# A hybrid decoder layer on one core: disjoint token halves in the up projection, with the halo of the convolution computed by ScalarE

## The chip, the cores and the metric

The kernel runs on one core of a Trainium2 chip. The metric is the device time of one execution in microseconds (us); the time of a kernel is the median of several executions.

## The reference, cut to what matters

One decoder layer on 1024 tokens, with 16 meta tokens ahead of them, in float32. Attention and a recurrent mixer come first; their output is added to the residual h. What the change touches is the ConvFFN behind them: an up projection to 2 x 2816 channels, a causal depthwise convolution over three tokens, GELU times the other half, and a down projection.

```python
def conv_ffn(a, w_up, conv_w, conv_b, w_down):
    u = a @ w_up
    u = lax.conv_general_dilated(
        u, conv_w[:, None, :], window_strides=(1,), padding=[(CONV_WIDTH - 1, 0)], ...) + conv_b
    gate, up = jnp.split(u, 2, axis=-1)
    return (jax.nn.gelu(gate, approximate=True) * up) @ w_down
...
    a = rmsnorm(h, ln_ffn_pre[l])
    y = conv_ffn(a, w_ffn_up[l], ffn_conv_w[l], ffn_conv_b[l], w_ffn_down[l])
    h = h + rmsnorm(y, ln_ffn_post[l])
return h[:, N_META:, :]
```

Only the 1024 tokens are returned. The first of them needs u of the two tokens before it, so the up projection runs on 1026 columns: the last two meta tokens and the 1024 tokens.

## The kernel before, in words

The layer runs in stages: attention and mixer, output projection, up projection with convolution, down projection. Each float32 operand of a matmul is split into a rounded part (hi, made by a cast on ScalarE) and the rest (lo, made by a subtraction on VectorE or GpSimd), and each product is three matmuls: hi x hi, hi x lo, lo x hi. All elementwise instructions are recorded through a helper, so in the profile their line is L59; they are told apart by the names of their tiles. TensorE's order is that of the code. The other engines' instructions are put in order by a scheduler; each engine then works through its own queue strictly in that order, waiting on semaphores.

**The up projection.** The channels are cut into 22 blocks of 128 for the gate and 22 for the other half; `ft` counts them. The 1026 columns are cut into two units, `p` = 0 and 1, and each unit's columns into a left and a right half. Round 0 (`plain_unit`, L1392) multiplies directly. Each of the rounds 1 to 21 (`unit`, L1410, driven by the loop at L1544) takes the 2 x 2 blocks (gate and other half by the two halves of the 1024 input features; the two halves of the columns) by a scheme with 7 products instead of 8. A product has 12 matmuls: four blocks of 128 input features by three parts. The products are numbered j = 0 to 6, and in each j unit 0 goes first and unit 1 follows.

- Before the rounds, `t_sums` (L1290) makes the sums of column blocks that products 1, 2, 3 and 5 read, in place in `at2`; `t_split` (L1279) splits the seven into the tiles `t`.
- `prep` (L1163) loads the four weight blocks of the next round (`ra`), makes their four sums on GpSimd (`ws`) and splits all seven into `uh` (cast on ScalarE) and `ul` (subtraction on VectorE or GpSimd). One weight is prepared in each j.
- Product 0 goes into the PSUM bank `pa`; ScalarE copies it to `xu` (x1). Products 1, 3 and 5 add up in the bank `pb`, 2 and 6 in `pc`, and 4 adds to `pa`. Between products VectorE reads the banks: behind product 1 it makes u2 (second half of `xu`) from pb and x1, behind product 3 it makes u3 (tile `u`) from pb and x1 and then a half of `uu`, and later the other halves of `uu` and `ug`. So product 5 may begin only when VectorE has read pb for `u`.
- `gated` (L1385) runs a round later, for unit 0 in j = 1 and for unit 1 in j = 3. It convolves `ug` and `uu` (`conv`, L1376): one ACTIVATE on ScalarE makes tap 2 and the bias, two scalar_tensor_tensor on VectorE add taps 1 and 0 in the tile `c`. GELU on ScalarE, a product on GpSimd and a store to DRAM (`gsc`) follow.

**The columns before the change.** Unit 0 has columns 0 to 515 (two halves of 258), unit 1 columns 514 to 1025 (two halves of 256). The two columns 514 and 515 are in both, since the convolution of unit 1 begins two columns late: unit 0 gives 514 tokens, unit 1 gives 510.

Of the kernel before, what the change touches and what calls it, by code (L numbers as in the profile page):

```python
# [9 lines left out]
F32 = mybir.dt.float32  # L10
F32R = mybir.dt.float32r
# [6 lines left out]
P = 128  # L18
# [11 lines left out]
NEG = -3.0e38  # L30
GROUPS = [(0, 3), (3, 6), (6, 9)]
WN = [258, 256]
C0 = [0, 514]
FA, FH, FO = 840, 800, 740
WR = 4
WARM = 26
# [55 lines left out]
def layer_kernel(ctx: ExitStack, tc: tile.TileContext, x, meta, xt, relative, lbl, gpre, gpost, win,  # L92
# [1162 lines left out]
    def trans(i):  # L1255
        r, t0 = tok(i)
        a2 = a2t.pop(i)
        cs = slice(t0 - 14, t0 - 14 + r)
        for half in range(2):
            pt = ps_b(f"pa2_{i}_{half}")  # L1260
            for j in range(4):
                k = 4 * half + j
                T.transpose(pt[:, j * r:(j + 1) * r], a2[:r, P * k: P * (k + 1)], ident[:r, :r])
            pv = pt[:, : 4 * r].rearrange("p (k t) -> p k t", k=4)
            ks = slice(4 * half, 4 * half + 4)
            for p in range(2):
                lo_, hi_ = max(cs.start, C0[p]), min(cs.stop, C0[p] + 2 * WN[p])
                if lo_ < hi_:
                    A.copy(
                        at2[p][:, ks, lo_ - C0[p]:hi_ - C0[p]], pv[:, :, lo_ - cs.start:hi_ - cs.start])  # L1270

    tt = [[None] * 8 for _ in range(2)]

    def t_tiles(p, j, where, tag):
        tag, n, off = (tag + (8 * WN[p], 0)[len(tag) - 1:])[:3]
        both = where.tile([P, n], F32R, tag=tag, name=f"t{p}_{j}")[:, off:off + 8 * WN[p]].rearrange("p (a c) -> p a c", a=8)
        return both[:, 0:4], both[:, 4:8]

    def t_split(p, j, src, where, *tag):  # L1279
        hi, lo = t_tiles(p, j, where, tag)  # L1280
        marks["cast"] = A.copy(hi, src)
        marks["low"] = V.tensor_tensor(lo, src, hi.bitcast(F32), op=ALU.subtract)
        tt[p][j] = (hi, lo)

    def quarter(p, j):
        n = WN[p]
        a, c = {0: (0, 0), 7: (0, n), 4: (4, 0), 6: (4, n)}[j]
        return at2[p][:, a:a + 4, c:c + n]

    def t_sums(p, where, last):  # L1290
# [24 lines left out]
    for i in range(1, NBLK):  # L1315
        py = ps_b(f"py1_{i}")
        if i >= 3:
            marks["gain"] = y0_gain(i)
        if i == 1:
            load_xh(1)  # L1320
            load_xh(0)
        if i + 1 < NBLK:
            for n in range(i + 1 if i < 6 else i + 2, min(i + 2 if i < 5 else i + 3, NBLK)):
                second_load(n)
            load_xh(i + 1)
        run(blocks[i], py, wo, range(4), True, False)
        if i == 3:
            trans(1)
        run(blocks[i], py, wo, range(4, 7 if i == 1 else 8), False, i > 1)
        if i > 3:  # L1330
            trans(i - 2)
        if i == 5:
            trans(0)
        if i == 1:
            pm = ps_b("py1_0")
            for _ in meta_part(pm, wo, True):
                pass
            for p in range(3):
                out_last(p)
            run(k7(1), py, wo[KD - 1:], range(1), False, True)  # L1340
            post(1, py)
            ysum = xhs.pop("sum")
            for l in range(2):
                A.copy(ysum[:2, 512 * l:512 * l + 512], pm[32 * l:32 * l + 2])
            G.tensor_tensor(ysum[:2, :512], ysum[:2, :512], ysum[:2, 512:], op=ALU.add)
            for p in (3, 4):
                out_last(p)
            continue
        post(i, py)
        if i == 2:  # L1350
            post(0, ysum[:, :512], ysum[:, 512:])
        if i == 5:
            t_split(0, 0, quarter(0, 0), ep, "e0")
            t_split(0, 4, quarter(0, 4), ep, "e1")
        if i == 7:
            with tc.issue_after(marks["scale"].ins), tc.issue_after(marks["normed"].ins):
                t_split(0, 7, quarter(0, 7), mxp, "X2", MIX["X2"])
        if i == 8:
            t_split(0, 6, quarter(0, 6), mxp, "X1", MIX["X1"], 16)
        if i in (2, 3):  # L1360
            for p in (1 + 2 * i, 2 + 2 * i):
                out_last(p)
# [22 lines left out]
    def gated(ft, p, ug, uu):  # L1385
        cg = conv(ft, p, 0, ug)
        A.activation(cg, cg, AF.Gelu_apprx_tanh)
        cu = conv(ft, p, 1, uu)
        marks["mult"] = G.tensor_tensor(cg, cg, cu, op=ALU.mult)
        marks["store"] = SY.dma_start(gsc[P * ft: P * (ft + 1), C0[p]:C0[p] + 2 * WN[p] - 2], cg)  # L1390

    def plain_unit(p, bank):  # L1392
        n = WN[p]
        us = outputs(0, p)
        for col in range(2):
            for side in range(2):
# [9 lines left out]
                A.copy(us[side][:, col * n:(col + 1) * n], pt)  # L1406
                yield
        later.append((0, p, *us))

    def unit(ft, p, bank):  # L1410
# [6 lines left out]
        x1, u2 = pair[:, :n], pair[:, WN[0]:WN[0] + n]  # L1417
        u3 = xup.tile([P, WN[0]], F32, tag="u3", name=f"u3_{nm}")[:, :n]

        def mm(j, pt, first):  # L1420
            hi, lo = made[7 * ft + j]
            th, tl = tt[p][j]
            for k in range(4):
                s = slice(P * k, P * (k + 1))
                T.matmul(pt, hi[:, s], th[:, k], start=(first and k == 0), stop=False, skip_group_check=True)  # L1425
                T.matmul(pt, hi[:, s], tl[:, k], start=False, stop=False, skip_group_check=True)  # L1426
                T.matmul(pt, lo[:, s], th[:, k], start=False, stop=(k == 3), skip_group_check=True)  # L1427
# [347 lines left out]
```

## Time and profile before

| | |
|---|---|
| median of three runs | 1270.1 us (1269.75 to 1271.96) |
| profiled execution | 1270.04 us |
| its span, first to last instruction | 1268.2 us |
| mean granted TensorE clock | 0.999 |
| busy: TensorE, VectorE, ScalarE, GpSimd | 99%, 72%, 54%, 40% |
| up projection, rounds 1 to 21 | about 636 to 1048 us of the span |

How to read the rows quoted below. In a timeline, a row begins with the start in us from the span's start and the duration, then engine (PE is TensorE, DVE VectorE, ACT ScalarE, POOL GpSimd, SPq SyncE's DMA queue), line, operation, the tiles it writes and reads (out<-in), shapes and types, and how many alike were merged. In brackets stand the engine's idle time ahead of it and the instruction that, by the profile, ended the wait. Successive instructions of an engine are pipelined, so one can start a little before the last has ended. A matmul is shown with 0.28 us, though the next starts much sooner; starts, not durations, tell its cost.

### The profile page before, as it was taken

Reading aid. Unit: us, or ns where it says so; the run is one execution under the profiler, and the core shown is the slowest. Engines: PE = TensorE matmul, PEld = TensorE weight load, DVE = VectorE, ACT = ScalarE, POOL = GpSimd, SP = SyncE. Lnnn points to the kernel's source line nnn. Section 1 sums busy time; section 2 is a strip of 40 time slices with the busy share of each in tenths; the row PEclk is TensorE's granted clock in tenths of the full one; section 3 lists DMA queues with packets and bytes.
Section 4 is the critical chain, followed back from the end, with each engine's and each line's share of the span. In section 5 each row is a group of like instructions: output and inputs, shape, how many; then the busy total and the mean of one; then the engine's idle time right before and its main releaser. Section 6 shows DMA issues by size and latency. Waiting matters only on the chain.

```text
span 1268.2 us, 26069 instructions
## 1 busy us (share of the span) xinstructions
PE 1254.6 (99%) x10168; PEld 1174.9 (93%) x10168; DVE 912.7 (72%) x1504; ACT 685.4 (54%) x1632; POOL 512.0 (40%) x396
## 2 busy tenths in 40 slices
PE   9999999999999999999999999999999999999997
PEld 8999999999999998778999999999999998878886
DVE  6764646565655564558899888889898877797586
ACT  7765466547644763456764544544445544564554
POOL 5442323333213311353067677677676731020111
PEclk9999999999999999999999999999999999999999
DMA  8554564464633534787222222222222247955363
GB/s 322 170 104 100 98 140 83 98 125 118 115 99 68 125 94 128 237 278 273 85 76 72 80 92 68 92 92 68 92 77 75 76 136 259 343 184 167 92 216 125
DMA packets 117599, 169.30 MB, mean 133 GB/s; under 512 B 10258, under 2 KB 57938, under 8 KB 117476
## 3 DMA queue, kind: packets, MB, share of 16 engines
q1 hardware_dynamic: 94244, 156.10, 37.7%
q0 software_dynamic: 23232, 11.54, 7.7%
q8 instruction: 80, 1.31, 0.4%
q14 instruction: 43, 0.35, 0.1%
HBM read 138.50 MB, written 52.17 MB: 150 GB/s over the span
## 4 chain that ended last, share of the span: by engine, by line
PE 83%; DMA 6%; DVE 4%; ACT 3%; issue 1%; POOL 1%; SPq 1%; DVEq 0%; ACTq 0%; POOLq 0%
PE pb L1426 5%; PE pb L1425 5%; PE pb L1427 4%; PE pd L1600 4%; PE pd L1601 4%; PE pd L1599 4%; PE pa L759 3%; PE pa L1426 3%; PE pc L1426 3%; PE pa L1425 3%; PE pc L1425 3%; PE pc L1427 3%; PE pa L1427 3%; DMA ra<-in_wup_dram 2%; PE pt L735 2%; DMA gi<-gsc 1%
## 5 line engine op out<-in xcount | busy, mean ns | idle before, releaser
L1425 PE MATMUL pb<-t,uh 128*128 128x258 f32 x504 | 140.6, 279 | 0.8 <-DVE u L59 0.8
L1426 PE MATMUL pb<-t,uh 128*128 128x258 f32 x504 | 140.9, 280 | 0.3 <-DVE t L59 0.3
L1427 PE MATMUL pb<-t,ul 128*128 128x258 f32 x504 | 140.1, 278 | 0.0
L1600 PE MATMUL pd<-wl,gh 128*128 128x512 f32 (+1 forms) x312 | 121.0, 388 | 1.2 <-DVE wl L59 1.2
L1599 PE MATMUL pd<-wh,gh 128*128 128x512 f32 (+1 forms) x312 | 120.8, 387 | 0.5 <-DVE x L59 0.5
L1601 PE MATMUL pd<-wh,gl 128*128 128x512 f32 (+1 forms) x312 | 120.7, 387 | 0.0
L59 DVE SCALAR_TENSOR_TENSOR c<-uu,cwt,c 128x514 f32<-128x514 f32 (+1 forms) x88 | 106.9, 1215 | 0.0
L59 DVE SCALAR_TENSOR_TENSOR c<-ug,cwt,c 128x514 f32<-128x514 f32 (+1 forms) x88 | 101.5, 1154 | 0.0
L59 ACT ACTIVATE c<-c 128x514 f32<-128x514 f32 (+1 forms) x44 | 27.9, 634 | 130.1 <-DVE c L59 130.1
L1425 PEld LDWEIGHTS pb<-t,uh 128*128 128x128 f32 x504 | 94.8, 188 | 1.0 <-DVE u L59 1.0
L1426 PEld LDWEIGHTS pb<-t,uh 128*128 128x128 f32 x504 | 94.8, 188 | 0.6 <-DVE t L59 0.6
L1427 PEld LDWEIGHTS pb<-t,ul 128*128 128x128 f32 x504 | 94.8, 188 | 0.0
L1426 PE MATMUL pa<-t,uh 128*128 128x258 f32 (+1 forms) x336 | 93.9, 279 | 0.0
L1426 PE MATMUL pc<-t,uh 128*128 128x258 f32 (+1 forms) x336 | 93.9, 279 | 0.0
L1425 PE MATMUL pa<-t,uh 128*128 128x258 f32 (+1 forms) x336 | 93.6, 279 | 0.0
L1425 PE MATMUL pc<-t,uh 128*128 128x258 f32 (+1 forms) x336 | 93.6, 278 | 0.0
L1427 PE MATMUL pa<-t,ul 128*128 128x258 f32 (+1 forms) x336 | 93.4, 278 | 0.0
L1427 PE MATMUL pc<-t,ul 128*128 128x258 f32 (+1 forms) x336 | 93.4, 278 | 0.0
L59 POOL TENSOR_TENSOR ul<-ws,uh 128x512 fp32r<-128x512 f32 x42 | 69.2, 1647 | 59.6 <-PE pa L1427 43.9
L59 POOL TENSOR_TENSOR ws<-ra,ra 128x512 f32<-128x512 f32 x42 | 67.8, 1615 | 61.0 <-DMA ra<-in_wup_dram 33.9
L59 POOL TENSOR_TENSOR c<-c,c 128x514 f32<-128x514 f32 (+1 forms) x44 | 68.5, 1558 | 54.2 <-ACT c L59 49.5
L59 DVE TENSOR_TENSOR ul<-ra,uh 128x512 fp32r<-128x512 f32 x43 | 41.6, 967 | 46.6 <-POOL ul L59 46.6
(386 smaller groups left out, 4179.8 us busy)
## 6 DMA issues: line engine op xcount, KB each, us to landing
ra<-in_wup_dram SPq DMA_DIRECT2D x88, 256.0 KB, 2.6
mp<-msc SPq DMA_DIRECT2D x23, 512.0 KB, 5.6
tsc<-in_wdown_dram SPq DMA_DIRECT2D x44, 256.0 KB, 5.6
wi<-tsc SPq DMA_DIRECT2D x44, 256.0 KB, 3.0
gi<-gsc SPq DMA_DIRECT2D x33, 256.0 KB, 4.0
wi<-in_wdown_dram SPq DMA_DIRECT2D x33, 256.0 KB, 5.3
gsc<-c SPq DMA_DIRECT2D x22, 257.0 KB, 2.0
tsc<-in_wdown_dram POOLq DMA_DIRECT2D x22, 256.0 KB, 6.7
```

Of the source, the lines that this page charges most:

```text
L59: ins = call(*args, **kw)
L735: T.transpose(pt[:b, jj * r:(jj + 1) * r], pb[:r, 0, start(j):start(j) + b], ident[:r, :r])
L759: T.matmul(po[:, :P], w_, vn[:, j], start=(j == 0), stop=(j == i))
L1425: T.matmul(pt, hi[:, s], th[:, k], start=(first and k == 0), stop=False, skip_group_check=True)
L1426: T.matmul(pt, hi[:, s], tl[:, k], start=False, stop=False, skip_group_check=True)
L1427: T.matmul(pt, lo[:, s], th[:, k], start=False, stop=(k == 3), skip_group_check=True)
L1599: T.matmul(py, gh[:, s], wh, start=(k == 0 and pr not in (3, 7)), stop=False, skip_group_check=True)
L1600: T.matmul(py, gh[:, s], wl, start=False, stop=False, skip_group_check=True)
L1601: T.matmul(py, gl[:, s], wh, start=False, stop=(k == NH - 1), skip_group_check=True)
```

## The change

The units become disjoint. Unit 0 now has columns 0 to 513, in a left half of 258 (two meta columns and 256 tokens) and a right half of 256; unit 1 has columns 514 to 1025 as before. The two meta columns take part only in the products that make left halves: 0, 1, 4 and 5. Products 2, 3 and 6 of unit 0 have 256 columns; product 3 adds into pb from its column 2. For the meta columns product 1 reads the same operand as product 0, so the split tile gets these columns as a copy (ScalarE); the operand of product 5 gets one small extra subtraction (VectorE, 4 x 2 columns). A few sizes of padding (`gap`) and offsets of tiles change with the narrower tiles.

Both units now give 512 tokens. For unit 1 the convolution needs the last two columns of unit 0, which are no longer among its own. Tap 2 and the bias run over all 512 columns; then three ACTIVATEs on ScalarE, each on a single column, add taps 1 and 0 of the missing columns from unit 0's `ug` or `uu` (`before`), with the column of `c` itself as the bias and the tap as the scale. VectorE's two steps start one and two columns later (511 and 510 columns). Unit 0's `ug` and `uu` are kept in `lefts` until then.

```diff
-C0 = [0, 514]
+C0 = [0, 514, 1026]
+HALF = 256
...
+    def width(p, j):
+        return WN[p] if j in (0, 1, 4, 5) else HALF
...
     def t_split(p, j, src, where, *tag):
-        hi, lo = t_tiles(p, j, where, tag)
+        hi, lo = tt[p][j] = t_tiles(p, j, where, tag)
+        o = width(p, j) - src.shape[-1]
+        if o:
+            for x, y in zip((hi, lo), tt[p][0]):
+                A.copy(x[:, :, :o], y[:, :, :o])
+        hi, lo = hi[:, :, o:], lo[:, :, o:]
...
         V.tensor_tensor(b21, b21, b22, op=ALU.subtract)
+        if o:
+            V.tensor_tensor(m21, m21, m11, op=ALU.subtract)
...
-    def conv(ft, p, side, u):
+    def conv(ft, p, side, u, before):
         m = ft + NF * side
-        w = 2 * WN[p] - 2
-        c = cv.tile([P, 514], F32, tag=f"c{side}", name=f"c{side}_{ft}_{p}", bufs=2 if side else 3)[:, :w]
-        A.activation(c, u[:, 2:2 + w], AF.Identity, bias=cbt[:, m:m + 1], scale=cwt[:, m, 2:3])
-        V.scalar_tensor_tensor(c, u[:, 1:1 + w], cwt[:, m, 1:2], c, ALU.mult, ALU.add)
-        V.scalar_tensor_tensor(c, u[:, 0:w], cwt[:, m, 0:1], c, ALU.mult, ALU.add)
+        c = cv.tile([P, 514], F32, tag=f"c{side}", name=f"c{side}_{ft}_{p}", bufs=2 if side else 3)[:, :512]
+        taps = [cwt[:, m, t:t + 1] for t in range(3)]
+        o = 2 * (p == 0)
+        A.activation(c, u[:, o:o + 512], AF.Identity, bias=cbt[:, m:m + 1], scale=taps[2])
+        if p:
+            for t, dst, src in ((1, 0, 1), (0, 0, 0), (0, 1, 1)):
+                d = c[:, dst:dst + 1]
+                A.activation(d, before[:, 512 + src:513 + src], AF.Identity, bias=d, scale=taps[t])
+        for t in (1, 0):
+            c0 = c[:, 2 - t - o if not o else 0:]
+            V.scalar_tensor_tensor(c0, u[:, t if o else 0:][:, :c0.shape[-1]], taps[t], c0, ALU.mult, ALU.add)
         return c
...
     def plain_unit(p, bank):
...
-                pt = bank(f"pq{p}_{col}{side}")[:, :n]
+                w = HALF if col else n
+                pt = bank(f"pq{p}_{col}{side}")[:, :w]
...
     def unit(ft, p, bank):
...
             th, tl = tt[p][j]
+            pt = pt[:, pt.shape[-1] - width(p, j):]
...
-        pc = bank(f"pc{nm}")[:, :n]
+        pc = bank(f"pc{nm}")[:, :HALF]
         mm(2, pc, True)
         yield
         mm(3, pb, False)
-        V.tensor_tensor(u3, pb, x1, op=ALU.add)
-        marks["last"] = V.tensor_tensor(uu[:, n:2 * n], pc, u3, op=ALU.add)
+        V.tensor_tensor(u3, pb[:, o:], x1[:, o:], op=ALU.add)
+        marks["last"] = V.tensor_tensor(uu[:, right], pc, u3, op=ALU.add)
```

On the chip's queues the rounds keep their order but for the small ACTIVATEs. This is ScalarE's queue of before, in the passage from round 5 to round 6, where the convolution of round 5 begins (`c`, then channel block and unit; `uh` is the cast of a weight, from a loaded block `ra` or a sum `ws`; `xu` is the copy of product 0 of round 6):

```order
L59 ACTIVATE c_5_0_9337<-uu_0_9007,cbt,cwt 128x514
L59 CAST uh_9224<-ws_9222 128x512
L59 ACTIVATE c_5_1_9418<-uu_1_9025,cbt,cwt 128x510
L59 ACTIVATE c_5_0_9332<-ug_0_9006,cbt,cwt 128x514
L59 CAST uh_9264<-ra_11_9254 128x512
L59 ACTIVATE c_5_1_9413<-ug_1_9024,cbt,cwt 128x510
L59 COPY xu_0_9270<-pa_0_9272 128x258
L59 CAST uh_9345<-ws_9343 128x512
L59 COPY xu_1_9288<-pa_1_9290 128x256
```

The same passage of ScalarE's queue with the change:

```order
L60 ACTIVATE c_5_0_9368<-uu_0_9032,cbt,cwt 128x512
L60 CAST uh_9255<-ws_9253 128x512
L60 ACTIVATE c_5_1_9452<-uu_1_9050,cbt,cwt 128x512
L60 ACTIVATE c_5_1_9452<-uu_0_9032,c_5_1_9452,cwt 128x1 x3
L60 ACTIVATE c_5_0_9363<-ug_0_9031,cbt,cwt 128x512
L60 CAST uh_9295<-ra_11_9285 128x512
L60 ACTIVATE c_5_1_9444<-ug_1_9049,cbt,cwt 128x512
L60 ACTIVATE c_5_1_9444<-ug_0_9031,c_5_1_9444,cwt 128x1
L60 COPY xu_0_9301<-pa_0_9303 128x258
L60 ACTIVATE c_5_1_9444<-ug_0_9031,c_5_1_9444,cwt 128x1 x2
L60 CAST uh_9376<-ws_9374 128x512
L60 COPY xu_1_9319<-pa_1_9321 128x256
```

Three small ACTIVATEs stand ahead of the second pair of convolutions and of the cast from `ra`, one ahead of the first copy to `xu`, two ahead of the next cast; nothing else has moved. VectorE's queue at the same place, with the change (`ul` is the rest of a weight, `u` is u3; the first copies to `xu` here are u2):

```order
L60 TENSOR_TENSOR uu_0_9032<-pb_0_9067,xu_0_9033 128x258
L60 TENSOR_TENSOR uu_1_9050<-pb_1_9081,xu_1_9051 128x256
L60 TENSOR_TENSOR ug_0_9031<-pc_0_9116,xu_0_9033 128x256
L60 TENSOR_TENSOR ug_1_9049<-pc_1_9129,xu_1_9051 128x256
L60 TENSOR_TENSOR ul_9296<-ra_11_9285,uh_9295 128x512
L60 TENSOR_TENSOR xu_0_9301<-pb_0_9335,xu_0_9301 128x256
L60 TENSOR_TENSOR ul_9377<-ws_9374,uh_9376 128x512
L60 TENSOR_TENSOR xu_1_9319<-pb_1_9349,xu_1_9319 128x256
L60 SCALAR_TENSOR_TENSOR c_5_0_9363<-ug_0_9031,cwt,c_5_0_9363 128x512
L60 SCALAR_TENSOR_TENSOR c_5_0_9368<-uu_0_9032,cwt,c_5_0_9368 128x512
```

Here the order is that of before, row for row; only widths differ (258 and 514 before where 256 and 512 stand now). The two `ul` wait for the casts of `uh` in ScalarE's queue above, and the two `xu` for ScalarE's copies.

More of the change, by code (lines that the diff above doesn't have):

```diff
@@ L1266, in trans @@
             for p in range(2):
-                lo_, hi_ = max(cs.start, C0[p]), min(cs.stop, C0[p] + 2 * WN[p])
+                lo_, hi_ = max(cs.start, C0[p]), min(cs.stop, C0[p + 1])
                 if lo_ < hi_:
@@ L1272, in layer_kernel @@
     tt = [[None] * 8 for _ in range(2)]
+    def width(p, j):
+        return WN[p] if j in (0, 1, 4, 5) else HALF
     def t_tiles(p, j, where, tag):
-        tag, n, off = (tag + (8 * WN[p], 0)[len(tag) - 1:])[:3]
-        both = where.tile([P, n], F32R, tag=tag, name=f"t{p}_{j}")[:, off:off + 8 * WN[p]].rearrange("p (a c) -> p a c", a=8)
+        w = width(p, j)
+        tag, n, off = (tag + (8 * w, 0)[len(tag) - 1:])[:3]
+        both = where.tile([P, n], F32R, tag=tag, name=f"t{p}_{j}")[:, off:off + 8 * w].rearrange("p (a c) -> p a c", a=8)
         return both[:, 0:4], both[:, 4:8]
     def t_split(p, j, src, where, *tag):
-        hi, lo = t_tiles(p, j, where, tag)
+        hi, lo = tt[p][j] = t_tiles(p, j, where, tag)
[4 more added lines that the diff above has]
+        hi, lo = hi[:, :, o:], lo[:, :, o:]
         marks["cast"] = A.copy(hi, src)
         marks["low"] = V.tensor_tensor(lo, src, hi.bitcast(F32), op=ALU.subtract)
-        tt[p][j] = (hi, lo)
     def quarter(p, j):
         n = WN[p]
-        a, c = {0: (0, 0), 7: (0, n), 4: (4, 0), 6: (4, n)}[j]
-        return at2[p][:, a:a + 4, c:c + n]
+        a, c, w = {0: (0, 0, n), 7: (0, n, HALF), 4: (4, 0, n), 6: (4, n, HALF)}[j]
+        return at2[p][:, a:a + 4, c:c + w]
     def t_sums(p, where, last):
         b11, b12, b21, b22 = (quarter(p, j) for j in (0, 7, 4, 6))
+        o = WN[p] - HALF
+        m11, m21, b11, all21, b21 = b11[:, :, :o], b21[:, :, :o], b11[:, :, o:], b21, b21[:, :, o:]
         cast, low = marks["quarters"]
@@ L1297, in t_sums @@
         for j, b in ((1, b22), (2, b11), (3, b12)):
-            if p == 0:
-                gap(where, f"gap4{j}", 128 if j == 1 else 192)
+            if p == 0 and j < 3:
+                gap(where, f"gap4{j}", 128 if j == 1 else 320)
             with nullcontext() if p or j == 1 else tc.issue_after(cast.ins):
@@ L1302, in t_sums @@
                     t_split(p, j, b, where, f"t{p}_{j}")
+        if p == 0:
+            gap(where, "gap43", 192)
         V.tensor_tensor(b21, b21, b22, op=ALU.subtract)
+        if o:
+            V.tensor_tensor(m21, m21, m11, op=ALU.subtract)
         with nullcontext() if p else tc.issue_after(cast.ins):
             with nullcontext() if p else tc.issue_after(low.ins):
-                t_split(p, 5, b21, *last)
+                t_split(p, 5, all21, *last)
     def run(*args):
@@ L1405, in plain_unit @@
                         T.matmul(pt, lo[:, s], th[:, k], start=False, stop=(kh == 1 and k == 3))
-                A.copy(us[side][:, col * n:(col + 1) * n], pt)
+                A.copy(us[side][:, col * n:col * n + w], pt)
                 yield
@@ L1416, in unit @@
         pair = mxp.tile([P, 768], F32, tag="ms", name=f"xu_{nm}", bufs=2)
-        x1, u2 = pair[:, :n], pair[:, WN[0]:WN[0] + n]
-        u3 = xup.tile([P, WN[0]], F32, tag="u3", name=f"u3_{nm}")[:, :n]
+        o = n - HALF
+        right = slice(n, n + HALF)
+        x1, u2 = pair[:, :n], pair[:, WN[0]:WN[0] + HALF]
+        u3 = xup.tile([P, WN[0]], F32, tag="u3", name=f"u3_{nm}")[:, :HALF]
         def mm(j, pt, first):
@@ L1434, in unit @@
         mm(1, pb, True)
-        marks[ft, p] = marks["last"] = V.tensor_tensor(u2, pb, x1, op=ALU.add)
+        marks[ft, p] = marks["last"] = V.tensor_tensor(u2, pb[:, o:], x1[:, o:], op=ALU.add)
         yield
-        pc = bank(f"pc{nm}")[:, :n]
+        pc = bank(f"pc{nm}")[:, :HALF]
         mm(2, pc, True)
@@ L1450, in unit @@
         mm(6, pc, False)
-        marks["last"] = V.tensor_tensor(ug[:, n:2 * n], pc, u2, op=ALU.add)
+        marks["last"] = V.tensor_tensor(ug[:, right], pc, u2, op=ALU.add)
         if ft < NF - 1:
```

14 lines of the change are left out of this document (9 added, 5 removed).

## Prediction

> **What bounds the kernel now.** I began with the page.
>
> ```profile
> PE 1254.6 (99%) x10168; PEld 1174.9 (93%) x10168; DVE 912.7 (72%) x1504; ACT 685.4 (54%) x1632; POOL 512.0 (40%) x396
> ```
>
> TensorE (PE) is busy nearly all the time, so it looks like the bound, and the change makes some of its matmuls narrower. The share is a mean over stages, though, so next I read the windows of the up projection (here 700 to 800 us; the columns are length, PE, PEld, DVE, ACT, POOL, granted clock, DMA share, GB/s).
>
> ```profile
> 700.00:800.00 100.00, 100.00 (x862) 100.00 (x861) 85.53 (x113) 49.13 (x92) 71.40 (x47) 1.00 0.25 81
> ```
>
> PE never waits here and VectorE (DVE) is 86% busy. What a narrower matmul is worth shows in the timeline of PE: a product of 12 matmuls on 258 columns, then one on 256.
>
> ```profile
> 802.29 0.28 PE L1425 MATMUL pb<-t,uh 128*128 128x258 f32 x1
> ...
> 803.73 0.28 PE L1425 MATMUL pb<-t,uh 128*128 128x256 f32 x1
> ...
> 805.09 0.28 PE L1425 MATMUL pa<-t,uh 128*128 128x258 f32 x1
> ```
>
> 1.44 us against 1.36: two columns cost 0.08 us a product. Then I asked how close the next engine is. The timeline of DVE over one of the 21 rounds (a round is one ft, both units):
>
> ```profile
> 736.12 0.75 DVE L59 TENSOR_TENSOR uu<-pb,xu 128x258 f32<-128x258 f32 x2
> 736.79 0.75 DVE L59 TENSOR_TENSOR ug<-pc,xu 128x258 f32<-128x258 f32 x2
> 739.98 1.27 DVE L59 TENSOR_TENSOR ul<-ra,uh 128x512 fp32r<-128x512 f32 x1 [2.45 <-POOL ul L59]
> 741.17 0.41 DVE L59 TENSOR_TENSOR xu<-pb,xu 128x258 f32<-128x258 f32 x1
> 741.51 0.68 DVE L59 TENSOR_TENSOR ul<-ws,uh 128x512 fp32r<-128x512 f32 x1
> 742.11 0.41 DVE L59 TENSOR_TENSOR xu<-pb,xu 128x256 f32<-128x256 f32 x1
> 742.44 0.74 DVE L59 SCALAR_TENSOR_TENSOR c<-ug,cwt,c 128x514 f32<-128x514 f32 x1
> ...
> 746.14 1.77 DVE L59 TENSOR_TENSOR ul<-ws,uh 128x512 fp32r<-128x512 f32 x1
> 747.84 0.41 DVE L59 TENSOR_TENSOR u<-pb,xu 128x258 f32<-128x258 f32 x1
> ...
> 759.33 1.27 DVE L59 TENSOR_TENSOR ul<-ra,uh 128x512 fp32r<-128x512 f32 x1 [2.45 <-POOL ul L59]
> ```
>
> DVE runs without a gap from 739.98 to about 757, then is idle 2.45 us, and starts over 19.35 us after the last time. The idle time is credited to POOL, which was done earlier. ScalarE (ACT) shows what ends it:
>
> ```profile
> 736.63 0.82 ACT L59 ACTIVATE c<-uu,cbt,cwt 128x514 f32<-128x514 f32 x1 [0.77 <-DVE uu L59]
> 737.36 0.60 ACT L59 CAST uh<-ws 128x512 fp32r<-128x512 f32 x1
> 737.86 0.81 ACT L59 ACTIVATE c<-uu,cbt,cwt 128x510 f32<-128x510 f32 x1
> 738.58 0.81 ACT L59 ACTIVATE c<-ug,cbt,cwt 128x514 f32<-128x514 f32 x1
> 739.29 0.60 ACT L59 CAST uh<-ra 128x512 fp32r<-128x512 f32 x1
> 739.80 0.82 ACT L59 ACTIVATE c<-ug,cbt,cwt 128x510 f32<-128x510 f32 x1
> 740.52 0.35 ACT L59 COPY xu<-pa 128x258 f32<-128x258 f32 x1
> 740.77 0.62 ACT L59 CAST uh<-ws 128x512 fp32r<-128x512 f32 x1
> ```
>
> The first uu on DVE ends at 736.53, ACT starts at 736.63, works without a gap, ends the cast of uh at 739.89, and DVE starts on ul at 739.98. So DVE and ACT form a loop: 16.9 us of DVE, then 2.45 us of ACT that DVE can't hide. It closes in 19.35 us.
>
> How close is that to PE? PE's own round, from two starts of product 5 of unit 0 in rounds 2 and 20:
>
> ```profile
> 670.94 0.37 PE L1425 MATMUL pb<-t,uh 128*128 128x258 f32 x1
> ```
>
> ```profile
> 1022.97 0.28 PE L1425 MATMUL pb<-t,uh 128*128 128x258 f32 x1
> ```
>
> 352.03 / 18 = 19.56 us. The loop has 0.21 us to spare in a round. And it does hold PE when it is late: product 5 adds into the bank pb, which DVE must have read for u:
>
> ```profile
> 670.45 0.41 DVE L59 TENSOR_TENSOR u<-pb,xu 128x258 f32<-128x258 f32 x1
> ```
>
> u ended at 670.86 and PE went on at 670.94. So in round 2 DVE is already as late as it may be, and from there it gains 0.21 us a round on PE.
>
> **The change part by part.** *Narrower products.* Unit 0 has 3 of 7 products on 256 columns instead of 258, in 21 rounds: 63 x 0.08 = 5.0 us of PE; two of four outputs of the plain unit add 4 x 0.08 = 0.3. PE's round becomes 19.56 - 0.24 = 19.32 us.
>
> *DVE.* The same instructions in the same order in every round, 0 to 4 columns narrower or wider (0.41 us at 258 and at 256): nothing. One subtraction of 4x2 columns and two small copies on ACT before the rounds: 0.1 to 0.5 us, once, taken at 0.3. The stores are 512 columns each, two fewer or more, in the same places of their queue: nothing. Unit 0's ug and uu are held two products longer, until unit 1's convolution has read them; their buffers are written again a round later at the earliest: nothing.
>
> *The halo on ACT.* Each convolution of unit 1 gets three ACTIVATEs on one column, so six a round, and the order shows where: three behind the second c<-uu, one behind the second c<-ug, two behind the first copy of xu. All stand inside the chain above. No row shows one element with two pointer operands. From below:
>
> ```profile
> 605.80 0.29 ACT L59 ACTIVATE ssy<-ssy,eps 128x1 f32<-128x1 f32 x1
> 606.13 0.20 ACT L59 ACTIVATE ssy<-ssy 128x1 f32<-128x1 f32 x1
> 606.24 0.58 ACT L59 ACTIVATE junk<-py 128x512 f32<-128x512 f32 x1
> ```
>
> Without a pointer it takes 0.20 and the next instruction starts 0.11 later; with one, 0.29. Where the second needs the first's result it starts 0.04 after its end. On 512 columns, two pointers make 0.81 of the cast's 0.60: 0.1 each. So my estimate is 0.39 long and 0.30 from start to start, with 0.11 (no pointer) and 0.43 (each waiting for the last) as ends. The Trainium skill (ScalarE: Activation LUTs, What ACT_TABLE_LOAD costs) has 186 ns for an ACTIVATE, 93 more per pointer operand and an overlap of 93; by it the estimate would be 0.28 from start to start and the time some 2 us less than mine.
>
> The chain anew, from the rows above. The second c<-uu ends at 738.67; the first small one needs its result: 738.71. With 0.30 each, c<-ug starts at 739.61 instead of 738.58 (1.03 later), the cast ends at 740.92, ul starts at 741.01. There DVE gets something back:
>
> ```profile
> 739.41 1.29 POOL L59 TENSOR_TENSOR ws<-ra,ws 128x512 f32<-128x512 f32 x1
> 744.10 1.57 POOL L59 TENSOR_TENSOR ws<-ra,ra 128x512 f32<-128x512 f32 x1 [3.40 <-DMA ra<-in_wup_dram]
> ```
>
> ul took 1.27 beside a POOL instruction and 0.68 without one; POOL is now done at 740.70, so ul takes 0.68 and ends at 741.69. ACT goes on: second c<-ug 740.83 to 741.65, one small one at 741.69, xu at 741.99 to 742.34, two small ones at 742.24 and 742.54, the cast 742.84 to 743.46. DVE can start its next ul at 743.55 instead of 741.51, and the first convolution step at 744.48 instead of 742.44: **2.04 us later**.
>
> From there to the next uu DVE has no idle time that could absorb it. It does share time with POOL: the ul at 746.14 takes 1.77 us, the one at 741.51 took 0.68; in all, five steps of that stretch are stretched so by about a POOL instruction each. POOL's next block waits for a load that SyncE issues behind that first ul:
>
> ```profile
> 741.28 0.33 SPq L1156 DMA_DIRECT2D ra<-in_wup_dram  x1
> ```
>
> It came 2.82 us later; now 741.69 + 0.03 + 2.82 = 744.54, just with the convolution. The same six POOL instructions meet the same DVE steps, in other pairs; I take their cost as equal, and one pairing more or less, 1.03 us, as the uncertainty. The loop is 19.35 + 2.04 = **21.39 us** against PE's 19.32: PE waits 2.07 us a round for u, ahead of product 5.
>
> *The sum*, by the start of product 5 against before. Round 2: +2.04, since u has no slack there. Rounds 3 to 19: 17 x (21.39 - 19.56) = 31.1. In round 20 POOL has no sums left to make for a next round:
>
> ```profile
> 1015.18 0.75 DVE L59 SCALAR_TENSOR_TENSOR c<-ug,cwt,c 128x514 f32<-128x514 f32 x1
> ...
> 1019.91 1.04 DVE L59 TENSOR_TENSOR ul<-ws,uh 128x512 fp32r<-128x512 f32 x1 [0.95 <-issue]
> 1020.88 0.42 DVE L59 TENSOR_TENSOR u<-pb,xu 128x258 f32<-128x258 f32 x1
> ```
>
> From the convolution to u it is 5.70 - 0.95 = 4.75 us instead of 747.84 - 742.44 = 5.40: +1.83 - 0.65 = 1.2. In round 21 no u is late any more: -0.2. With the 0.3 of before the rounds: 34.4 us. The down projection has the same work; six small instructions stand ahead of its first casts, 0 to 2 us, taken at 0, since by the same timeline DVE waits for PE in round 21. The profiled execution took 1270.04 us (span 1268.2), the median is 1270.1: **1304.4 us**. The narrower matmuls earn nearly nothing, since PE waits for what they save.
>
> Ends: 0.11 a small instruction gives 0.92 in place of 2.04, a loop of 20.27 and 1283 us; 0.43 gives 2.84, 22.19 and 1320; one POOL pairing less or more gives 1285 or 1324.
>
> **The rivals.** *PE stays the bound, faster.* DVE idles longer, so POOL may finish more of its work there. Each step that escapes POOL gives 1.03 us back; the point from which it decides is two of the five in every round: then the loop is 19.33 and PE gets its 5.3 us: 1264.7. For it: 2 us more idle time on DVE, and POOL only 71% busy. Against it: POOL's next block hangs on the load behind ul and can't use the gap. 0.11.
>
> *The products are not cheaper*, because the 0.08 comes with where a row starts or is written (product 3 now writes from column 2 of its bank), not with the width; and the loop has slack as in the rival before. Then the time is 1270, no change. Against it: unit 1 shows 1.36 at 256. 0.05. The Trainium skill (TensorE: Matmul & The Clock Gate, Wait — 56ns, not 53.3ns?) says that matmuls follow each other at N / 2.4 GHz plus 2.5 ns, so two columns would be 0.01 us a product; the rows above show 0.08 and do not bear it out.
>
> *POOL collides more*, with two more pairings a round: 23.4 us, 1343. The load would have to land at the worst moment each time. 0.04.
>
> **How the numbers follow.** My forecast has 0.80, with its own range from 1283 to 1324 by the ends above; rounded outward that is the range, and leaves out the two first rivals and the last. 0.2% is 2.5 us, about the spread of the runs of before (1269.75 to 1271.96). Faster 0.11, same 0.05, slower 0.84.
>
> **What would show it.** In the profile after: DVE's idle time before ul<-ra near 3.5 us instead of 2.45, and two new gaps of some 0.6 us behind it; ul there at 0.68; PE idle about 2 us a round before the first matmul of pb, released by u; rounds of 21.4 us; products of unit 0 on 256 columns at 1.36. It is wrong if PE has no gaps in the up projection, if the small ACTIVATEs stand off the chain, or if DVE's steps beside POOL become fewer.

## The result, and the profile after

The changed kernel takes 1308.9 us (median of five runs, 1307.2 to 1309.8), the kernel before 1271.8 in the same session: 1.0294 of it, 95% interval 1.0279 to 1.0309. It is slower by 37 us. The profiled execution took 1307.18 us, with a span of 1305.4.

The first line of the page and the window of the up projection that the prediction showed of before:

```profile
PE 1261.1 (97%) x10168; PEld 1180.5 (90%) x10168; DVE 906.0 (69%) x1505; ACT 720.6 (55%) x1764; POOL 501.5 (38%) x396
```

```profile
700.00:800.00 100.00, 94.09 (x799) 93.50 (x798) 74.70 (x103) 52.07 (x111) 61.28 (x42) 0.98 0.23 74
```

The whole-span shares hardly move (PE 99% to 97%). In the stage, PE falls from 100.00 to 94.09 and DVE from 85.53 to 74.70: nobody is busy all the time any more, the mark of a loop of waits between engines. What PE waits for stands in its group of the page (first matmul of the bank pb; last columns: idle time and what ended it):

```profile
L1455 PE MATMUL pb<-t,uh 128*128 128x258 f32 (+1 forms) x504 | 146.1, 290 | 28.7 <-DVE u L60 28.7
```

The timeline of ACT in one passage between two rounds, the queue that the section on the change listed:

```profile
810.29 0.82 ACT L60 ACTIVATE c<-uu,cbt,cwt 128x512 f32<-128x512 f32 x1
811.14 0.94 ACT L60 ACTIVATE c<-uu,c,cwt 128x1 f32<-128x1 f32 x3
811.99 0.80 ACT L60 ACTIVATE c<-ug,cbt,cwt 128x512 f32<-128x512 f32 x1
812.70 0.60 ACT L60 CAST uh<-ra 128x512 fp32r<-128x512 f32 x1
813.21 0.81 ACT L60 ACTIVATE c<-ug,cbt,cwt 128x512 f32<-128x512 f32 x1
814.05 0.39 ACT L60 ACTIVATE c<-ug,c,cwt 128x1 f32<-128x1 f32 x1
814.35 0.35 ACT L60 COPY xu<-pa 128x258 f32<-128x258 f32 x1
814.60 0.67 ACT L60 ACTIVATE c<-ug,c,cwt 128x1 f32<-128x1 f32 x2
815.17 0.61 ACT L60 CAST uh<-ws 128x512 fp32r<-128x512 f32 x1
```

ACT works through without a gap. A small ACTIVATE is 0.39 long; three take 0.94, so they follow each other at 0.28 ((0.94 - 0.39) / 2). The second c<-uu starts 1.70 ahead of c<-ug instead of 0.72. And DVE in the same passage:

```profile
813.39 0.69 DVE L60 TENSOR_TENSOR ul<-ra,uh 128x512 fp32r<-128x512 f32 x1 [3.43 <-POOL ws L60]
814.73 0.43 DVE L60 TENSOR_TENSOR xu<-pb,xu 128x256 f32<-128x256 f32 x1 [0.65 <-ACT xu L60]
815.88 0.69 DVE L60 TENSOR_TENSOR ul<-ws,uh 128x512 fp32r<-128x512 f32 x1 [0.72 <-ACT uh L60]
...
816.82 1.77 DVE L60 SCALAR_TENSOR_TENSOR c<-ug,cwt,c 128x512 f32<-128x512 f32 x1
818.51 1.78 DVE L60 SCALAR_TENSOR_TENSOR c<-uu,cwt,c 128x512 f32<-128x512 f32 x1
820.21 1.78 DVE L60 SCALAR_TENSOR_TENSOR c<-ug,cwt,c 128x512 f32<-128x512 f32 x1
821.91 0.74 DVE L60 SCALAR_TENSOR_TENSOR c<-uu,cwt,c 128x512 f32<-128x512 f32 x1
823.25 1.35 DVE L60 TENSOR_TENSOR ul<-ws,uh 128x512 fp32r<-128x512 f32 x1 [0.60 <-issue]
824.52 0.41 DVE L60 TENSOR_TENSOR u<-pb,xu 128x256 f32<-128x256 f32 x1
```

The idle time ahead of ul<-ra is 3.43 (2.45 before), behind it stand new gaps of 0.65 and 0.72, and this ul takes 0.69 instead of 1.27. The profile credits the wait at 813.39 to POOL, whose sum ended at 813.14; the cast on ACT ended later, at 813.30, just ahead of ul. From the first step of the convolution to the end of u it is now 8.11 us (816.82 to 824.93), where the prediction read 5.81 before; in the other half of the rounds it is 6.8, as the section on why shows.

PE's rounds, from the starts of product 5 of unit 0 in rounds 2 and 19:

```profile
673.76 0.39 PE L1455 MATMUL pb<-t,uh 128*128 128x258 f32 x1 [2.20 <-DVE u L60]
...
1039.97 0.58 PE L1455 MATMUL pb<-t,uh 128*128 128x258 f32 x1 [3.21 <-DVE u L60]
```

(1039.97 - 673.76) / 17 = 21.54 us a round, against 19.56. The narrower products are there: products 2 of unit 0 and of unit 1 and product 3 of unit 0 begin at

```profile
793.32 0.28 PE L1455 MATMUL pc<-t,uh 128*128 128x256 f32 x1
...
794.67 0.28 PE L1455 MATMUL pc<-t,uh 128*128 128x256 f32 x1
...
796.03 0.28 PE L1455 MATMUL pb<-t,uh 128*128 128x256 f32 x1
```

so each takes 1.35 or 1.36 us, and PE then waits for what they saved.

### The profile page after: what moved, and what is told of

It reads as the page before. It is cut to its first block, busy times and chain, and to the rows that moved or that the text cites. A ratio compares the mean times of both kernels' runs of the same rounds, so it can differ in the third digit from the quotient of the medians.

```text
span 1305.4 us, 26214 instructions
## 1 busy us (share of the span) xinstructions
PE 1261.1 (97%) x10168; PEld 1180.5 (90%) x10168; DVE 906.0 (69%) x1505; ACT 720.6 (55%) x1764; POOL 501.5 (38%) x396
## 5 line engine op out<-in xcount | busy, mean ns | idle before, releaser
L1455 PE MATMUL pb<-t,uh 128*128 128x258 f32 (+1 forms) x504 | 146.1, 290 | 28.7 <-DVE u L60 28.7
L1456 PE MATMUL pb<-t,uh 128*128 128x258 f32 (+1 forms) x504 | 144.7, 287 | 0.8 <-DVE t L60 0.8
L1457 PE MATMUL pb<-t,ul 128*128 128x258 f32 (+1 forms) x504 | 144.1, 286 | 0.0
L60 ACT ACTIVATE c<-c 128x512 f32<-128x512 f32 x44 | 27.8, 633 | 187.2 <-DVE c L60 187.2
L1455 PEld LDWEIGHTS pb<-t,uh 128*128 128x128 f32 x504 | 99.0, 196 | 31.8 <-DVE u L60 31.7
L60 DVE SCALAR_TENSOR_TENSOR c<-ug,cwt,c 128x512 f32<-128x512 f32 (+1 forms) x88 | 113.1, 1286 | 0.0
L60 DVE SCALAR_TENSOR_TENSOR c<-uu,cwt,c 128x512 f32<-128x512 f32 (+1 forms) x88 | 105.5, 1199 | 0.0
L60 POOL TENSOR_TENSOR c<-c,c 128x512 f32<-128x512 f32 x44 | 68.3, 1553 | 89.6 <-ACT c L60 74.0
L1456 PEld LDWEIGHTS pb<-t,uh 128*128 128x128 f32 x504 | 99.1, 197 | 1.0 <-DVE t L60 1.0
L1455 PE MATMUL pc<-t,uh 128*128 128x256 f32 x336 | 93.1, 277 | 0.0
L1456 PE MATMUL pc<-t,uh 128*128 128x256 f32 x336 | 93.1, 277 | 0.0
L1457 PE MATMUL pc<-t,ul 128*128 128x256 f32 x336 | 93.0, 277 | 0.0
L1630 PEld LDWEIGHTS pd<-wl,gh 128*128 128x128 f32 x312 | 58.6, 188 | 14.6 <-DVE wl L60 2.9
```

The costliest lines, as they stand in the source:

```text
L60: ins = call(*args, **kw)
L1630: T.matmul(py, gh[:, s], wl, start=False, stop=False, skip_group_check=True)
```

## The experiments

The theory: six small ACTIVATEs a round stand in a chain that DVE waits for, and this alone makes the loss. The rivals: the narrower products, new columns or longer held tiles bring it; POOL's collisions with DVE (steps of both that stretch each other) bring it; PE's clock behind its waits has a part in it. Times are medians, ratios are to runs of the kernel before on the same chip, with 95% intervals; rounds are means from round 2 to round 19, by the starts of product 5.

### 1. No halo

```diff
-        if p:
-            for t, dst, src in ((1, 0, 1), (0, 0, 0), (0, 1, 1)):
-                d = c[:, dst:dst + 1]
-                A.activation(d, before[:, 512 + src:513 + src], AF.Identity, bias=d, scale=taps[t])
```

> The changed kernel without the six small ACTIVATEs of a round (the first two tokens of unit 1's convolution lack the taps of the columns before them). Theory, the small ACTIVATEs in the chain between DVE and ACT are the whole loss: the chain closes in 19.35 us again and PE's narrower round takes 19.32, so 1270.0 - 17 x 0.21 + 0.3 = about 1266.5 us (1264 to 1269), DVE idle about 2.45 us ahead of ul<-ra, and PE without a wait ahead of product 5. Rival, the loss comes from the narrower products, the new columns or the tiles that are held longer: over 1290 us, with PE still waiting for u about 2 us a round. Rival, POOL collides more with DVE: part of the loss stays, 1275 to 1295.

This kernel leaves out the taps of the two columns ahead of unit 1. 1268.1 us, ratio 0.9972 (0.9962 to 0.9982). In the stage:

```profile
700.00:1000.00 300.00, 300.00 (x2605) 299.83 (x2605) 258.26 (x344) 144.31 (x268) 212.06 (x139) 1.00 0.26 84
```

PE is busy through, the rounds are 19.36 us. Widths, new columns and held tiles are all still in this kernel, so none of them costs anything that can be seen; 41 us hang on the small ACTIVATEs.

### 2. The halo alone, on the kernel before

```diff
-        V.scalar_tensor_tensor(c, u[:, 1:1 + w], cwt[:, m, 1:2], c, ALU.mult, ALU.add)
-        V.scalar_tensor_tensor(c, u[:, 0:w], cwt[:, m, 0:1], c, ALU.mult, ALU.add)
+        if p:
+            for t, dst, src in ((1, 0, 1), (0, 0, 0), (0, 1, 1)):
+                d = c[:, dst:dst + 1]
+                A.activation(d, u[:, src:src + 1], AF.Identity, bias=d, scale=cwt[:, m, t:t + 1])
+        for t in (1, 0):
+            o = (2 - t) * p
+            V.scalar_tensor_tensor(c[:, o:], u[:, t + o:t + w], cwt[:, m, t:t + 1], c[:, o:], ALU.mult, ALU.add)
```

> The kernel before, with its own overlapping columns and full widths, but with the six small ACTIVATEs of a round in the same places (here they read unit 1's own ug and uu, whose first two columns hold the same values), and DVE's two steps starting one and two columns later. Theory: the chain is that of the changed kernel, so its time too, about 1309 us (1305 to 1312), since what the narrower products save is only waited for; PE's waits ahead of product 5 are 0.24 us shorter than in the changed kernel. Rival, the narrowing or the longer held tiles bring a part of the loss: 1270 to 1295 us.

1310.1 us, ratio 1.0314 (1.0289 to 1.0339), rounds of 21.52 us. The same loss without the rest of the change: in the changed kernel the narrower products earn nothing that shows beside the noise.

### 3. The halo, off the chain

```diff
         if p:
-            for t, dst, src in ((1, 0, 1), (0, 0, 0), (0, 1, 1)):
-                d = c[:, dst:dst + 1]
-                A.activation(d, before[:, 512 + src:513 + src], AF.Identity, bias=d, scale=taps[t])
+            with tc.issue_after(marks["x1"].ins):
+                for t, dst, src in ((1, 0, 1), (0, 0, 0), (0, 1, 1)):
+                    d = c[:, dst:dst + 1]
+                    A.activation(d, before[:, 512 + src:513 + src], AF.Identity, bias=d, scale=taps[t])
```

`issue_after` sets only the place in ScalarE's queue: behind the copy named by the mark.

> The changed kernel, complete, with the six small ACTIVATEs queued behind ScalarE's copy xu of unit 1, where ScalarE has idle time ahead of GELU. Theory: it is the place that costs, not the instructions; the chain is 19.35 us again, PE 19.32, and the time about 1266.5 us (1264 to 1270). Rival, the instructions cost wherever they stand, because the casts and GELU behind them come 1.8 us later and DVE then waits for one of those: the loop stays near 21 us and the time near 1300 us.

1267.8 us, ratio 0.9967 (0.9954 to 0.9980): a complete kernel that is faster than before. ACT:

```profile
762.03 0.37 ACT L60 COPY xu<-pa 128x256 f32<-128x256 f32 x1
762.29 0.95 ACT L60 ACTIVATE c<-ug,c,cwt 128x1 f32<-128x1 f32 x3
763.14 0.94 ACT L60 ACTIVATE c<-uu,c,cwt 128x1 f32<-128x1 f32 x3
763.97 0.61 ACT L60 CAST uh<-ws 128x512 fp32r<-128x512 f32 x1
765.28 0.63 ACT L60 ACTIVATE c<-c 128x512 f32<-128x512 f32 x1 [0.70 <-DVE c L60]
```

The six take the same 1.7 us as ever, and behind them ACT is still idle for 0.70 ahead of GELU: cover enough. DVE has its old row back:

```profile
760.72 1.27 DVE L60 TENSOR_TENSOR ul<-ra,uh 128x512 fp32r<-128x512 f32 x1 [2.46 <-POOL ul L60]
```

It is the place of the instructions that costs, not the instructions.

### 4. Unit 1's long ACTIVATEs off the chain as well

```diff
-        A.activation(c, u[:, o:o + 512], AF.Identity, bias=cbt[:, m:m + 1], scale=taps[2])
+        with tc.issue_after(marks["x1"].ins) if p else nullcontext():
+            A.activation(c, u[:, o:o + 512], AF.Identity, bias=cbt[:, m:m + 1], scale=taps[2])
```

with the edit of the third experiment.

> As the last, and unit 1's two long ACTIVATEs of the convolution also stand behind the copies xu. Theory: the cast of uh from ra comes 0.7 us earlier than in the kernel before, the loop is about 18.6 us at most, PE is the bound at 19.32 a round, and the narrower products bring what they save: 1270.0 - 5.3 + 0.3 = about 1265 us (1263 to 1268), DVE idle ahead of ul<-ra for PE's sake. Rival, ScalarE becomes late for the cast behind GELU, or POOL for the product: 1270 us or more.

1267.1 us, ratio 0.9962 (0.9948 to 0.9976), the fastest version, though its interval overlaps that of the third. DVE:

```profile
796.11 0.69 DVE L60 TENSOR_TENSOR ul<-ra,uh 128x512 fp32r<-128x512 f32 x1 [1.74 <-issue]
797.62 0.42 DVE L60 TENSOR_TENSOR xu<-pb,xu 128x256 f32<-128x256 f32 x1 [0.82 <-PE pb L1459]
```

The wait for ACT is shorter by 0.71 and DVE now waits for PE. PE's rounds are 19.33 us from round 3 on.

### 5. Half the halo

```diff
-        if p:
+        if p and side:
```

> The changed kernel with the three small ACTIVATEs of uu alone (those of ug are left out, so that half of the channels lack the taps of the columns before unit 1). Theory, each small ACTIVATE in the chain costs its 0.3 us: of the 2.04 us a round 1.03 are left, the loop takes 20.4 us and PE waits about 1.05 us in every round; the time is 1270 + 1.0 + 17 x (20.4 - 19.56) + 0.5 = about 1286 us (1282 to 1292). All waits are then shorter than those behind which PE went on at half its clock, so the rounds are even and the granted clock is 1.00. Rival, the loss is a step (for example a POOL instruction that meets another one of DVE's): the time is near that of the changed kernel, over 1300, or near that of before, under 1275.

This kernel leaves out those taps for one half of the channels. 1289.8 us, ratio 1.0152 (1.0137 to 1.0167), inside the range, 4 us above the 1286 us of the theory. The rounds are 20.29 us, nearly all within 0.03 of each other, and the granted clock of the stage is 1.00. Of the 4 us, 2.3 are one wait of PE for a cast (gh) in the down projection, at 1084.5 us, that the traces of before and after don't have. Each small ACTIVATE takes its 0.3 us from every round: (20.29 - 19.36) / 3 = 0.31. It is no step.

### 6. Twice the halo

```diff
-            for t, dst, src in ((1, 0, 1), (0, 0, 0), (0, 1, 1)):
+            for t, dst, src in ((1, 0, 1), (0, 0, 0), (0, 1, 1)) * 2:
```

> The changed kernel with each of the six small ACTIVATEs done twice (the first two tokens of unit 1 get those taps twice). Theory: 6 x 0.30 = 1.8 us more in the chain of each round, a loop of about 23.3 us, 1309 + 18 x 1.8 = about 1341 us (1333 to 1350), waits of PE near 4 us in every round, and half the clock behind each of them, which the next wait hides. Rival, PE's slow clock has a price of its own: then each round has 1.7 us more and the time is over 1360 us. Rival, the instructions behind the first six find idle time: under 1330 us.

1328.9 us, ratio 1.0455 (1.0441 to 1.0468): a miss of the theory. It lies just under the 1330 us of the rival by which the later instructions find idle time, and ACT shows that some of them do:

```profile
820.86 0.81 ACT L60 ACTIVATE c<-ug,cbt,cwt 128x512 f32<-128x512 f32 x1
821.57 0.37 ACT L60 ACTIVATE c<-uu,c,cwt 128x1 f32<-128x1 f32 x1
...
822.11 1.22 ACT L60 ACTIVATE c<-ug,c,cwt 128x1 f32<-128x1 f32 x4
823.23 0.35 ACT L60 COPY xu<-pa 128x256 f32<-128x256 f32 x1
823.48 0.62 ACT L60 CAST uh<-ws 128x512 fp32r<-128x512 f32 x1
824.00 0.39 ACT L60 ACTIVATE c<-ug,c,cwt 128x1 f32<-128x1 f32 x1
```

The scheduler placed the instructions anew. With the three behind c<-uu only eight of the twelve stand ahead of the cast that DVE waits for, and four behind it; in addition the second copy of xu has slipped ahead of the cast. So the cast begins 2.62 us behind the start of the second c<-ug (820.86 to 823.48) instead of 1.96 (813.21 to 815.17), 0.66 more. The rest is POOL's: from the convolution to the end of u it takes 8.1 us in every round from 2 to 19 but one, which in the changed kernel only every other round does, and such a round is some 0.2 us longer than the mean (see the section on why). By the starts of ul<-ra the rounds are 22.37 us against 21.46, and the two make up these 0.9. By the start of product 5 in round 21 that makes 16.4 us; one more wait of the kind seen in the fifth experiment, 4.4 us in the down projection, makes most of the rest. The expectation counted instructions, not places; those that stand behind the cast are free, as in the third experiment.

### 7. More work for PE

```diff
                 T.matmul(pt, lo[:, s], th[:, k], start=False, stop=(k == 3), skip_group_check=True)
+            if (p, j) == (1, 4) and 3 <= ft <= 19:
+                for k in range(8):
+                    s = slice(P * (k % 4), P * (k % 4 + 1))
+                    T.matmul(pt, lo[:, s], th[:, k % 4], start=False, stop=(k == 7), skip_group_check=True)
```

> The changed kernel, with eight more matmuls of 256 columns behind product 4 of unit 1 in the rounds 3 to 19 (they add parts of product 4 to its bank a second time, so the output is not the reference's). They take 0.9 us of PE just ahead of its wait for u, so the waits are at most 2.6 us instead of 3.5, and fewer of them, or none, are followed by matmuls at half the clock. Theory, the loop between DVE and ACT sets the time and PE has 2 us to spare: no change, 1309 us (1307 to 1311), though PE has 17 x 0.9 = 15 us more work. Rival, PE's slow stretches delay the loop (a round takes 21.54 us where the chain alone gives 21.39): 1309 - 17 x 0.15 = 1306 us, faster with more work. Rival, PE is the bound all the same: 1309 + 15 = 1324 us.

The added matmuls add parts of product 4 a second time; only their time matters here. 1308.1 us, ratio 1.0292 (1.0278 to 1.0306), the ratio of the changed kernel (1.0294) with 17 x 0.9 us more matmuls. The group of PE that waits:

```profile
L1455 PE MATMUL pb<-t,uh 128*128 128x258 f32 (+1 forms) x504 | 143.8, 285 | 17.6 <-DVE u L60 17.6
```

The added work, 15 us, went into the waits (28.7 to 17.6) and into the time that fewer stretches at half the clock left free (three in the rounds instead of six). The rounds are 21.51 us. PE is not the bound, and no cost of its slow stretches can be seen. The changed kernel says the same: in its longer rounds, ul<-ra starts again after 21.66 to 21.72 us with a slow stretch between and after 21.68 to 21.81 us without.

### 8. The long ACTIVATEs late, with the widths of before

```diff
-        A.activation(c, u[:, 2:2 + w], AF.Identity, bias=cbt[:, m:m + 1], scale=cwt[:, m, 2:3])
+        with tc.issue_after(marks["x1"].ins) if p else nullcontext():
+            A.activation(c, u[:, 2:2 + w], AF.Identity, bias=cbt[:, m:m + 1], scale=cwt[:, m, 2:3])
```

> The kernel before, with unit 1's two long ACTIVATEs of the convolution behind the copies xu, as in the fastest version so far, but with the full widths. Theory: in the kernel before PE was the bound but for 0.2 us in round 2, so a shorter chain brings nothing there: 1271 us, within 0.2% of before (1269 to 1273), and the 4.6 us by which the version with both edits beat the kernel before are those of the narrower products. Rival, the shorter chain alone brings the gain: 1267 us.

1276.5 us, ratio 1.0041 (1.0028 to 1.0053): slower than before, a miss on both sides. DVE in one of its rounds, and POOL beside it:

```profile
839.17 0.43 DVE L59 TENSOR_TENSOR xu<-pb,xu 128x258 f32<-128x258 f32 x1 [1.03 <-ACT c L59]
...
840.89 1.74 DVE L59 SCALAR_TENSOR_TENSOR c<-ug,cwt,c 128x514 f32<-128x514 f32 x1
...
847.29 1.39 DVE L59 TENSOR_TENSOR ul<-ws,uh 128x512 fp32r<-128x512 f32 x1 [0.60 <-issue]
848.60 0.42 DVE L59 TENSOR_TENSOR u<-pb,xu 128x258 f32<-128x258 f32 x1
```

```profile
840.78 1.30 POOL L59 TENSOR_TENSOR ws<-ra,ra 128x512 f32<-128x512 f32 x1 [1.49 <-DMA ra<-in_wup_dram]
```

POOL's block of sums starts 0.11 us ahead of the convolution, which takes 8.13 us to the end of u (840.89 to 849.02). Where POOL starts ahead of the convolution or up to 0.03 us behind it, the next ul<-ra comes after 20.0 to 20.3 us; where it starts 0.05 us or more behind, after 19.5 to 19.6 in most rounds. The mean of PE's rounds is 19.79. So the shorter chain let ul and with it POOL's load come sooner, into the steps on which product 5 waits. That this is the cause is read from the trace; it wasn't tried by itself.

### 9. The late halo, with the widths of before

The kernel of the second experiment, with the three small ACTIVATEs queued as in the third.

> The kernel before with its own widths and with the six small ACTIVATEs of a round, but queued behind the copies xu: the twin of the complete changed kernel with the late halo, without the narrower products. Theory: the chain is that of before (19.35 us), the small ACTIVATEs lie in ScalarE's idle time, DVE's steps beside POOL are those of before, and PE is the bound with 19.56 us a round: 1271 us, within 0.2% of before (1269 to 1273). The 0.22 us a round to the version with narrower products, 20 x 0.22 = 4.5 us, is then what these are worth. Rival, the late halo itself changes how POOL meets DVE, as moving the long ACTIVATEs did in the wide kernel (conv to u in 6.8 to 8.2 us instead of 5.8): 1274 to 1280 us.

1271.5 us, ratio 1.0005 (0.9996 to 1.0013), rounds of 19.56 us: no change, as the theory has it. Beside the third experiment (0.9967, rounds of 19.35) it prices the narrower products where PE is the bound: 0.2 us a round, and by the ratios, each to the kernel before on its own chip, 0.0038 of the time, about 5 us.

## Why the prediction was right, point by point

**The mechanism** held. Taking the six instructions out of the chain gives the loss back (1, 3), putting them into the kernel before makes it (2), half of them make about half (5), and PE has time to spare (7).

**The small ACTIVATE**: 0.30 estimated, 0.28 to 0.30 measured (814.05 to 814.35 is 0.30, the row of three 0.28). By what the Trainium skill states (ScalarE: Activation LUTs, What ACT_TABLE_LOAD costs) the estimate was 0.28, and the rows of three agree.

**The rows foretold** came to within 0.1 us: idle time 3.43 (about 3.5), the gaps 0.65 and 0.72 (some 0.6), ul 0.69 (0.68), products of 1.36. One sign did not come as foretold: PE is not idle about 2 us in every round. In rounds 2 to 19 it waits for u 14 times, 27.8 us in all. Behind six of these waits it runs at half its clock for 3.4 us, and its product 5 of unit 0 with what follows up to product 1 of the next round takes 9.90 to 10.11 us instead of 8.31, some 10 us in all. In the rounds behind four of these (6, 10, 12 and 16) PE comes later than u and doesn't wait at all.

**The sum** was 34.4 us, the trace gives 37.2. Term by term, by the start of product 5:

| | predicted | measured |
|---|---|---|
| start and round 2 | 0.3 + 2.04 | 2.82 (673.76 against 670.94) |
| rounds 3 to 19 | 17 x 1.83 = 31.1 | 17 x 1.98 = 33.7 (rounds of 21.54, not 21.39) |
| rounds 20 and 21 | 1.2 - 0.2 | 1.2 |
| behind round 21 | 0 | -0.5 |

The 0.3 of the start can't be told: product 5 of round 1 begins 0.27 us later than before here, but anywhere from 651.5 to 654.9 us in the other runs with narrower products. The loop itself is read better from the ul that opens it, in rounds 2 and 19:

```profile
663.51 0.69 DVE L60 TENSOR_TENSOR ul<-ra,uh 128x512 fp32r<-128x512 f32 x1 [3.44 <-POOL ws L60]
...
1028.34 0.69 DVE L60 TENSOR_TENSOR ul<-ra,uh 128x512 fp32r<-128x512 f32 x1 [3.71 <-POOL ws L60]
```

(1028.34 - 663.51) / 17 = 21.46 us. The chain on ACT puts the convolution 1.95 us later (0.98 ahead of ul, and 3.43 instead of 2.46 us from ul to the convolution), where the prediction had 2.04; the other 0.16 is POOL's, where it had nothing. The 21.54 by product 5 contains another 1.4 us in 17 rounds, since u comes 6.76 us behind the start of the convolution in round 2 and 8.14 in round 19. That the forecast came within 5 us thus rests on the chain, and in small part on terms of opposite sign.

**The step that was off in size** is "the same six POOL instructions meet the same DVE steps, in other pairs; I take their cost as equal". The cost over a round is nearly equal, the place is not. POOL's block of sums (ws<-ra,ra, ul, ws<-ws,ra) began 1.66 us behind the convolution in the round of before that the prediction shows (744.10 against 742.44) and now begins with it, as the prediction had it; what it left out is what follows. This is DVE in round 2, where POOL came 0.18 us behind DVE's first step, then POOL:

```profile
666.94 0.74 DVE L60 SCALAR_TENSOR_TENSOR c<-ug,cwt,c 128x512 f32<-128x512 f32 x1
667.60 1.78 DVE L60 SCALAR_TENSOR_TENSOR c<-uu,cwt,c 128x512 f32<-128x512 f32 x1
669.31 1.77 DVE L60 SCALAR_TENSOR_TENSOR c<-ug,cwt,c 128x512 f32<-128x512 f32 x1
671.00 1.77 DVE L60 SCALAR_TENSOR_TENSOR c<-uu,cwt,c 128x512 f32<-128x512 f32 x1
672.69 0.68 DVE L60 TENSOR_TENSOR ul<-ws,uh 128x512 fp32r<-128x512 f32 x1
673.29 0.41 DVE L60 TENSOR_TENSOR u<-pb,xu 128x256 f32<-128x256 f32 x1
```

```profile
667.12 1.72 POOL L60 TENSOR_TENSOR ws<-ra,ra 128x512 f32<-128x512 f32 x1 [3.88 <-DVE xu L60]
```

Three stretched steps now lie ahead of u instead of two, so u comes 1 us later once, in round 2 (6.76 us from the convolution to the end of u, 5.81 before); behind u there is one fewer, and the loop of such a round is 21.2 us (the same ul a round earlier started at 792.19, 21.20 us ahead of 813.39). In the round shown in the first section POOL came 0.07 us ahead of DVE:

```profile
816.75 1.29 POOL L60 TENSOR_TENSOR ws<-ra,ra 128x512 f32<-128x512 f32 x1 [3.62 <-DMA ra<-in_wup_dram]
```

Then the first step is stretched and the fourth is not (0.74 at 821.91), and nothing covers the cast that stands behind GELU in ACT's queue any more: 0.60 us of a new wait ahead of ul at 823.25, and a loop of 21.7 (the next one starts at 835.08). The two kinds alternate from round 2 to round 19; the mean is the 21.46 us above. A wait that an earlier collision had covered was not in my sum. In these 18 rounds the first step is stretched where POOL starts ahead of it or up to 0.03 us behind, and is not where POOL starts 0.04 us or more behind; this is read from the trace and was not tried by itself. That so small a lead decides agrees with what the Trainium skill states (SBUF — State Buffer, Who interferes with whom): a step of VectorE with both inputs in SBUF and a GpSimd instruction that reads SBUF block each other, and the order of issue decides who waits. The steps of 1.77 beside a POOL instruction of 1.7 are such; the steps that read a bank of PSUM stay at 0.41 to 0.43.

**The rivals.** That POOL would lose collisions and PE stay the bound did not happen, nor did two more pairings a round; the nearest to it is the change of place above. The narrower products were cheaper as forecast; by 2 they are worth nothing that shows here, and by 3 and 9 about 5 us once the chain is free.

## What to carry to other kernels

An engine that is 54% busy can still hold the chain that sets the end: before putting an instruction into its queue, find what stands behind that place and who waits for it. Here 1.7 us of small instructions cost 2 us a round in one place and nothing a few rows further down the same queue. Where two engines stretch each other's steps, moving one of them may do more than shift the collisions: here it decided on which side of the critical step they fell, and laid bare a short wait that they had covered.

## What was not expected of the hardware

PE's clock. Behind some of its waits of 2.2 to 3.2 us PE goes on at half speed. The windows of one such place in the changed kernel, the stretch behind the wait and the wait itself:

```profile
739.50:742.90 3.40, 3.40 (x18) 3.40 (x17) 3.37 (x6) 0.00 (x0) 1.90 (x2) 0.51 0.46 127
735.50:739.20 3.70, 0.80 (x9) 0.60 (x7) 3.07 (x5) 2.45 (x5) 1.73 (x3) 1.00 0.02 8
```

The granted clock is 0.51 for 3.4 us, some 16 matmuls at 0.215 us. It happens behind six of the waits (rounds 2, 5, 9, 11, 15 and 19) and not behind others of the same length: not at 782.08 us, behind this one,

```profile
782.08 0.39 PE L1455 MATMUL pb<-t,uh 128*128 128x258 f32 x1 [2.38 <-DVE u L60]
```

while the wait of 2.20 in round 2 had it. The granted clock shows what tells them apart. The slow stretches begin at 674.70, 739.55, 824.89, 869.26, 954.59 and 1039.92 us, and the distances, 64.85, 85.33, 44.37, 85.33 and 85.33 us, are 19, 25, 13, 25 and 25 times 3.413 us. On a grid of that step, each of the six waits has 2.02 us or more within one window, and the slow stretch begins at that window's end; of the other waits none has more than 1.81 us within one (the one at 782.08 is cut into 1.57 and 0.81). The seventh experiment agrees: 2.08 to 2.21 us in one window ahead of its three slow stretches, at most 1.80 elsewhere. So the place of a wait on the grid decides along with its length.

The Trainium skill (TensorE: Matmul & The Clock Gate, What's actually happening) has a free-running window of about 3.4 us over which activity is judged, and the halved clock after at least one idle window. The length of the slow stretch and the grid agree with it. But a window that is idle for some 2 us of its 3.4 is enough here. In this kernel the slow stretch only shortens PE's next wait, or takes its place.
